# The u and v projections of a transformer mixer as one product in seven parts, with another order of the projections, the Fourier stage and attention

## The chip, the cores and the metric

The kernel runs on one core of a Trainium2 chip. The metric is the device time of one execution in microseconds (us). The engines are TensorE (PE, matmuls), VectorE (DVE), ScalarE (ACT), GpSimd (POOL, here an issuer of DMAs) and SyncE (SP, an issuer of DMAs). Each runs its own queue of instructions in order and waits on semaphores of the others. Matmuls write to eight banks of PSUM, 128 x 512 float32 each.

## The reference, cut to what matters

x is 512 x 1024 (512 tokens on an 8 x 64 grid). Two layers, each of them a half SwiGLU step, a mixer, and another half SwiGLU step; at the end a norm.

```python
def mixer(h, w_in, gate_bias, rpb, w_na_out, w_f_out, w_o):
    z = h @ w_in                     # h = rms_norm(x, g), 512 x 1024
    q, k, v, uf = z[..., :512], z[..., 512:1024], z[..., 1024:1536], z[..., 1536:2048]
    ga, gf = z[..., 2048:3072], z[..., 3072:]
    y_na = neighbourhood_attention(q, k, v, rpb) @ w_na_out   # 8 heads of 64, softmax over a window
    y_f = fourier_mix(uf) @ w_f_out  # per group of 128 channels: real part of the 2-D DFT
    g_na, g_f = sigmoid(ga + gate_bias[0]), sigmoid(gf + gate_bias[1])
    return (g_na * y_na + g_f * y_f) @ w_o
```

## The kernel before, in words

**Precision.** Every operand of a large matmul is split in a high part (in a rounded type, made by ACT, `hi`) and a low part (the rest, made by DVE, `lo`). A product is three matmuls: high by high, high by low, low by high. `mm3` (L285 to L288) is this for one tile; `late_low` (L439 to L450) puts the matmuls with the weights' low parts behind the others of a granule. `split` (L290 to L296) makes the two parts.

**Weights.** `Stream` and `Item` (from L151) bring the weights as granules of 128 x 1024 in a fixed order. SP loads a granule (`raw`), up to eight granules ahead (`FETCH`); some have a second granule added to them by an accumulating DMA of POOL or by a sum on DVE (L160). ACT makes `whi` (L175), DVE makes `wlo` (L178); three buffers each. `prep` stays two granules ahead of PE.

**Products in seven parts.** The feed-forward steps, the gates and the output projection split a 2 x 2 block product in Strassen's way: seven products of block sums in place of eight. A `product` (L447 to L450) takes two granules and writes a pair of PSUM banks: 24 matmuls of 512 columns. `snap` (L517) copies a pair of banks to SBUF on ACT, `less` (L522) subtracts such a copy on DVE. `ORDER` is the order 1, 5, 2, 6, 7, 3, 4.

**Norm.** The class `Norm` turns x by transposes (bank `tr`) and multiplies by the gain in four quads (`quad`: half of the channels by half of the tokens). The factor 1/rms of a token is `r` (`rstd`, L422 and L423, `rsqrt`, L304 to L309); it is applied after the products. `spread` writes r to DRAM and reads it back as a row on all partitions (`R`), which q and k need, since their tokens lie along the columns.

**The mixer** (`stage_mixer`), all in one order on PE:

- `proj_U`: u for the first 256 tokens, and for the last 256 tokens mirrored. For the mirror ACT and DVE copy the activations in reverse (`flip`, L986 and L987). 48 + 48 matmuls of 512 columns. Then sums and differences of the two halves, each split.
- `proj_V`: 96 matmuls of 512 columns in four banks, out by a split with r (L295, L296).
- `four_pos` four times: the Fourier transform along the positions, 12 matmuls of 256 columns each. DVE multiplies the bank by two rows of factors (L1048, L1049), adds and subtracts halves (L1050, L1051), and the result is split (L292, L293).
- `proj_q(0)`, `proj_k(0)`: `proj_T`, 24 matmuls of 512 columns each; DVE multiplies by R (L970), then a split (L292 and L293, or L295 and L296 for q).
- `four_ch` four times: the transform along the channels, two banks for each group, 6 matmuls. ACT copies the second bank (`fq`, L1063), DVE adds it to and takes it from the first (L1065, L1067), then a split (L1071, L1072).
- `proj_q(1)`, then for the head pairs `att_next`, `proj_k`, `att_outs`, `proj_q`: `att_next(hp)` transposes the probabilities of the pair before (L1140), makes the scores of this one (L1104), and calls `att_probs`: minimum of negated scores with the bias added on DVE (L1118), exponentials with sums on ACT (L1124), reciprocals on DVE (L1127), scaled copies on ACT (L1131).
- `f_some(n)`: n of the eight rows of the Fourier branch's output product, 12 matmuls each, which are put between the attention's parts.
- The gates and the output projection in seven parts each.

**What sets the order.** Within one engine the order is fixed when the program is built: a scheduler takes what is ready by its own estimate, except where `manual_schedule` keeps the order of the code for the named engines and `high_priority` draws a step ahead. [...] A pool gives out the banks of PSUM, and a matmul that starts a new content of a bank waits for the last reader of the old one. `constants` (L944) puts the loads of the Fourier matrices and factors on POOL's queue.

Of the kernel before, what the change touches and what calls it, by code (L numbers as in the profile page):

```python
# [40 lines left out]
def _granules():  # L41
# [7 lines left out]
    for l in range(L):  # L49
        for w in (1, 2):  # L50
# [36 lines left out]
def encoder_kernel(  # L87
# [95 lines left out]
    def stage_items():  # L183
# [5 lines left out]
        def strassen(s, name, idx, sizes, order, dma=False):  # L189
# [7 lines left out]
            for m in order:  # L197
                for g in range(len(sizes)):
# [7 lines left out]
                    elif m == 4:  # L206
                        add(d2[g])
                    elif m == 5:
                        add(d)
                    elif m == 6:  # L210
                        add(d, a, then=b.key if dma else None)
                    else:
                        add(c)

# [15 lines left out]
        for l in range(L):  # L230
# [4 lines left out]
            for name, n in (("u", 4), ("v", 4), ("qk", 8), ("f", 4)):  # L235
                for g in range(n):
                    add(Raw((s, name, g)))
# [11 lines left out]
    class Stream:  # L249
        def __init__(self):  # L250
            self.items = stage_items()
            self.pos = self.loaded = self.prepped = 0
            self.stage = 0

# [6 lines left out]
        def prep(self, to):  # L261
            n = len(self.items)
            while self.prepped < min(to, n) and self.items[self.prepped].stage <= self.stage:
                self.fetch(self.prepped + FETCH)
# [4 lines left out]
        def enter(self, stage):  # L269
            self.stage = stage  # L270
            self.fetch(self.prepped + FETCH)
# [40 lines left out]
    class Norm:  # L312
# [40 lines left out]
        def quad(self, i, j):  # L353
            self.tiles(i)
            js = slice(j * 256, (j + 1) * 256)
            hq, lq = self.h[i][:, :, js], self.l[i][:, :, js]
            if not self.mix:
                raw = self.raw[i, j] = slot(F32, "xr")
            for k2 in range(2):
# [11 lines left out]
            if not self.mix:  # L371
                split(hq, lq, raw)
# [45 lines left out]
        def rstd(self):  # L418
# [6 lines left out]
            if self.mix:  # L425
                pc = bank()
                PE.matmul(pc[:, 0:2], mirror, self.r[:, 3:1:-1], start=True, stop=True)
                self.rflip = small("rflip", 2)
                V.tensor_copy(self.rflip, pc[:, 0:2])
# [3 lines left out]
            V.tensor_tensor(self.r2, self.r, self.r, ALU.mult)  # L433

# [85 lines left out]
    def less(ps, t):  # L520
        for b in range(2):
            V.tensor_tensor(t[:, b, :], ps[b], t[:, b, :], ALU.subtract)  # L522

    def stage_ffn(norm, nxt, late):
# [27 lines left out]
        norm.tiles(1)  # L552
# [16 lines left out]
        acts = {1: (hx[0], lx[0], 0), 2: (hx[1], lx[1], 0), 3: (hx[1], lx[1], 256), 4: (*t4, 0)}  # L569

        def combine(m):

            if m == 5:
                V.tensor_tensor(raw[0, 0], raw[0, 0], raw[0, 1], ALU.subtract)
                acts[5] = parts(raw[0, 0], "t1")
            elif m == 7:
                V.tensor_tensor(raw[0, 1], raw[0, 1], raw[1, 1], ALU.subtract)
                acts[7] = parts(raw[0, 1], "t3")
            elif m == 6:
                V.tensor_tensor(raw[0, 0], raw[1, 1], raw[0, 0], ALU.add)  # L580
                acts[6] = parts(raw[0, 0], "t2")
            else:
                V.tensor_tensor(raw[1, 0], raw[1, 0], raw[0, 0], ALU.subtract)
                split(*t4, raw[1, 0])
# [230 lines left out]
        for i, (m, c, _) in enumerate(steps):  # L815
# [16 lines left out]
            if m == 4 and c == 0 and not late:  # L832
                with tc.manual_schedule(engines={mybir.EngineType.DVE, mybir.EngineType.Activation}):
                    make(i + 2)
                    nxt.quad(1, 1)
                    nxt.quad(0, 1)
# [94 lines left out]
    def stage_mixer(l, norm, nxt):  # L931
        mp = mix_pool[0]

# [22 lines left out]
        def wide():  # L956

            wh, wl = ws.next()
            for k in range(2):
                c = slice(k * T, (k + 1) * T)  # L960
                yield wh[:, c], wl[:, c]

        def proj_T(scale):
# [5 lines left out]
            t = tmp(s="q")  # L969
            V.tensor_tensor(t, ps, R, ALU.mult)  # L970
            hi, lo = hilo("q")
            split(hi, lo, t, scale)
            return hi, lo

        def proj_U():
            pss = [bank() for _ in range(4)]

            def straight(kt, wh, wl):
                for c in range(2):
                    lh, ll = [z[:, c * P : (c + 1) * P] for z in xs[kt]]  # L980
                    mm3(pss[c], lh, ll, wh, wl, kt == 0, kt == DT - 1)

            def mirrored(kt, wh, wl):
                flip = tmp(F32R, s="flip")
                xh, xl = [z.bitcast(F32) for z in xs[kt]]
                S.activation(flip[:, 0:256], xh[:, 511:255:-1], AF.Copy)  # L986
                V.tensor_copy(flip[:, 256:512], xl[:, 511:255:-1])  # L987
                for c in range(2):
                    lh, ll = [flip[:, z + c * P : z + c * P + P] for z in (0, 256)]
                    mm3(pss[2 + c], lh, ll, wh, wl, kt == 0, kt == DT - 1)  # L990

            for g in range(2):
                for k, w in enumerate(wide()):
                    straight(2 * g + k, *w)
                    mirrored(2 * g + k, *w)
                if g == 0:
                    norm.settle()
            w = [*wide(), *wide()]
            for kt in range(4):
                mirrored(4 + kt, *w[kt])  # L1000
            for kt in range(4):
                straight(4 + kt, *w[kt])
            norm.rstd()
            norm.spread(R)
# [645 lines left out]
```

## Time and profile before

| | |
|---|---|
| median of 3 runs | 1905.43 us (1904.45 to 1906.28) |
| profiled execution | 1906.04 us |
| its span in the trace | 1904.2 us |
| mean granted clock of PE | 0.999 |
| matmuls | 9189 |
| DMA | 364.36 MB, 191 GB/s over the span |
| mixer of layer 0: first matmul of u | 336.99 us |
| first position transform | 381.67 us |
| first scores | 406.76 us |
| first gate product | 492.51 us |

The span runs from the first to the last instruction in the trace; the profiled execution is the time of the same run from outside. In rows of the timeline the first number is the start in the span, the second the length of one instruction or group; matmuls overlap, so what a matmul costs is the distance to the next start. The end of a row says what ended the idle time ahead of it.

### The profile page before, as it was taken

The numbers are of one execution on the slowest core, as the hardware profiler recorded it, in microseconds if no ns is written. First come the engines' busy times: TensorE is split into PE (matmuls) and PEld (weight loads), VectorE is DVE, ScalarE is ACT, GpSimd is POOL, SyncE is SP. The second block draws the span as 40 slices with busy tenths as digits, with TensorE's granted clock in tenths as the row PEclk, the third lists the DMA queues.
The fourth block names the chain that finished last, engine by engine and source line by source line (L and its number), as shares of the span: only waits on it lengthen the run. The fifth ranks groups of instructions, "written<-read, shape, count | busy, mean of one in ns | idle before, by whom it ended". The sixth has DMA issues, their size and how long they took to land.

```text
span 1904.2 us, 25091 instructions
## 1 busy us (share of the span) xinstructions
PE 1891.7 (99%) x9189; PEld 1586.8 (83%) x9189; DVE 1602.4 (84%) x2000; ACT 1161.6 (61%) x1676; POOL 160.7 (8%) x198
## 2 busy tenths in 40 slices
PE   9999999999999999999999999999999999999998
PEld 7888888888888888888888888888888888888886
DVE  7877899586889987889997778995769899787899
ACT  6655665468566755566665556663675576555655
POOL 0101010000111010001010100100001101000010
PEclk9999999999999999999999999999999999999999
DMA  8776499323886776649877664992247867766594
GB/s 301 202 207 187 150 249 320 105 84 104 217 218 166 180 195 204 177 152 262 251 185 210 187 180 152 268 339 74 68 130 215 215 170 175 207 177 177 170 275 147
DMA packets 104636, 364.36 MB, mean 191 GB/s; under 512 B 12032, under 2 KB 12160, under 8 KB 104512
## 3 DMA queue, kind: packets, MB, share of 16 engines
q1 hardware_dynamic: 77568, 270.70, 40.1%
q0 software_dynamic: 26800, 92.04, 26.8%
q8 instruction: 72, 1.18, 0.2%
q14 instruction: 52, 0.43, 0.1%
q10 hardware_dynamic: 144, 0.02, 0.0%
HBM read 357.46 MB, written 2.11 MB: 189 GB/s over the span
## 4 chain that ended last, share of the span: by engine, by line
PE 95%; issue 2%; DMA 2%; DVE 1%; ACT 0%; POOL 0%; DVEq 0%; ACTq 0%; POOLq 0%; SPq 0%
PE A L447 9%; PE A L448 9%; PE A L450 9%; PE o L448 7%; PE o L447 7%; PE o L450 7%; PE ps L286 5%; PE ps L288 5%; PE ps L287 5%; PE B L448 4%; PE B L447 4%; PE B L450 4%; PE C L448 2%; PE C L447 2%; PE C L450 2%; PE tr L540 2%
## 5 line engine op out<-in xcount | busy, mean ns | idle before, releaser
L175 ACT ACTIVATE whi<-raw 128x1024 fp32r<-128x1024 f32 (+1 forms) x528 | 546.1, 1037 | 423.4 <-PE A L448 123.2
L178 DVE TENSOR_TENSOR wlo<-raw,whi 128x1024 fp32r<-128x1024 f32 (+1 forms) x528 | 627.3, 1193 | 191.2 <-ACT whi L175 186.5
L146 POOL DMA_DIRECT2D raw<-in_wst_dram x158 | 136.2, 873 | 1440.2 <-DMA raw<-in_wst_dram 674.7
L160 DVE TENSOR_TENSOR raw<-raw,raw 128x1024 f32<-128x1024 f32 (+1 forms) x146 | 172.6, 1191 | 1.2
L448 PE MATMUL A<-whi,xl 128*128 128x512 f32 x384 | 149.5, 389 | 0.0
L447 PE MATMUL A<-whi,xh 128*128 128x512 f32 x384 | 149.4, 389 | 0.0
L450 PE MATMUL A<-wlo,xh 128*128 128x512 f32 x384 | 110.5, 389 | 0.0
L170 ACT ACTIVATE whi<-raw 128x1024 fp32r<-128x1024 f32 (+1 forms) x79 | 81.6, 1036 | 40.2 <-PE A L448 12.4
L171 DVE SCALAR_TENSOR_TENSOR wlo<-raw,whi 128x1024 fp32r<-128x1024 f32 (+1 forms) x79 | 93.1, 1193 | 12.2 <-ACT whi L170 12.2
L633 ACT ACTIVATE th<-sn,rh 128x512 f32<-128x512 f32 x80 | 56.8, 714 | 69.4 <-DVE sn L522 69.4
L517 ACT ACTIVATE sn<-A 128x512 f32<-128x512 f32 x96 | 56.4, 589 | 51.3 <-PE A L450 51.2
L450 PEld LDWEIGHTS A<-wlo,xh 128*128 128x128 f32 x384 | 72.1, 188 | 15.0
L448 PEld LDWEIGHTS A<-whi,xl 128*128 128x128 f32 x384 | 72.1, 188 | 14.8
L447 PEld LDWEIGHTS A<-whi,xh 128*128 128x128 f32 x384 | 72.1, 188 | 14.8
L447 PE MATMUL B<-whi,t1h 128*128 128x512 f32 x192 | 76.2, 397 | 0.0
L447 PE MATMUL A<-whi,t3h 128*128 128x512 f32 x192 | 75.3, 392 | 0.4 <-ACT sn L517 0.4
L447 PE MATMUL C<-whi,xh 128*128 128x512 f32 x192 | 74.9, 390 | 0.0
L447 PE MATMUL A<-whi,t2h 128*128 128x512 f32 x192 | 74.9, 390 | 0.0
L448 PE MATMUL B<-whi,t1l 128*128 128x512 f32 x192 | 74.8, 390 | 0.0
L448 PE MATMUL A<-whi,t3l 128*128 128x512 f32 x192 | 74.8, 390 | 0.0
L448 PE MATMUL C<-whi,xl 128*128 128x512 f32 x192 | 74.7, 389 | 0.0
L448 PE MATMUL A<-whi,t2l 128*128 128x512 f32 x192 | 74.7, 389 | 0.0
(409 smaller groups left out, 4748.2 us busy)
## 6 DMA issues: line engine op xcount, KB each, us to landing
raw<-in_wst_dram SPq DMA_DIRECT2D x466, 512.0 KB, 5.4
raw<-in_wst_dram POOLq DMA_DIRECT2D x162, 512.0 KB, 7.9
raw<-in_wst_dram SPq DMA_DIRECT2D x30, 256.0 KB, 3.9
bm<-in_bias_dram SPq DMA_DIRECT2D x16, 384.0 KB, 6.0
vs<-v SPq DMA_DIRECT2D x12, 256.0 KB, 4.9
x<-in_xin_dram SPq DMA_DIRECT2D x4, 512.0 KB, 10.2
raw<-in_wst_dram POOLq DMA_DIRECT2D x8, 256.0 KB, 8.7
dft<-in_dft_dram POOLq DMA_DIRECT2D x8, 256.0 KB, 6.2
```

The costliest lines, as they stand in the source:

```text
L146: G.dma_start(out=self.t, in_=wst[GRAN_AT[self.plus]][:, 0 : self.n], accum_op=ALU.add)
L160: V.tensor_tensor(self.raw.t, self.raw.t, self.add.t, ALU.add)
L170: S.activation(hi, t, AF.Copy, scale=-1.0)
L171: self.last = V.scalar_tensor_tensor(lo, t, -1.0, hi.bitcast(F32), ALU.mult, ALU.subtract)
L175: S.activation(hi[:, cs], t[:, cs], AF.Copy)
L178: self.last = V.tensor_tensor(lo[:, cs], t[:, cs], hi[:, cs].bitcast(F32), ALU.subtract)
L286: PE.matmul(ps, lh, rh, start=start, stop=False, skip_group_check=again)
L287: PE.matmul(ps, lh, rl, start=False, stop=False, skip_group_check=again)
L288: PE.matmul(ps, ll, rh, start=False, stop=stop, skip_group_check=again)
L447: PE.matmul(ps, lh, rh, start=start, stop=False, skip_group_check=again)
L448: PE.matmul(ps, ll, rh, start=False, stop=False, skip_group_check=again)
L450: PE.matmul(ps, lh, rl, start=False, stop=stop, skip_group_check=again)
```

## The change

1. u and v are one block product in seven parts. The 2 x 2 blocks are halves of the channels by halves of the tokens on one side, and halves of the channels by (u, v) on the other. The granules `ua` to `ud` take the place of the eight granules of u and v. Order of the products: 1, 5, 6, 2, 7, 3, 4.
2. The granules of q0, k0 and q1 stand behind those of products 5, 6 and 2; PE computes these projections there. A projection now gives back a function for its second step (the product by R and the high part) and one for its third (the low part).
3. Inside `proj_UV`, DVE and ACT keep the order of the code. The low part of quad (0,1) is put off to after product 1.
4. The mirror is taken after the product: for each of two blocks, two matmuls of the split u (`uh`, `ul`) with a rounded mirror matrix.
5. k1 and q2 follow, then the position transforms, scores of pair 0, k2, the channel transforms, q3, and the rest of attention. Of the f rows, one stands ahead of `att_next(2)`, two and one around `att_outs(1)`, and one less on each side of `att_outs(3)`.
6. A quad now goes through float32 (`raw`) for the mixer too: four scaled copies on ACT, one conversion for the high part, one subtraction on DVE for the low.
7. `combos` holds the combinations of the feed-forward steps and of the mixer in common.

```diff
@@ stage_items @@
-            for name, n in (("u", 4), ("v", 4), ("qk", 8), ("f", 4)):
-                for g in range(n):
-                    add(Raw((s, name, g)))
+            qk = [(s, "qk", g) for g in range(8)]
+            strassen(s, lambda q: "u" + q, 0, two, (1, 5, 6, 2, 7, 3, 4), True, behind={5: qk[0:1], 6: qk[1:2], 2: qk[2:3]})
+            for key in qk[3:] + [(s, "f", g) for g in range(4)]:
+                add(Raw(key))
...
@@ Norm.quad_high @@
-                    if self.mix:
-                        split(hq[:, kt, :], lq[:, kt, :], tr[:, k, :], self.gain(4 * i + kt))
-                    else:
-                        S.activation(raw[:, kt, :], tr[:, k, :], AF.Copy, scale=self.gain(4 * i + kt))
-            if not self.mix:
-                split(hq, lq, raw)
+                    S.activation(raw[:, kt, :], tr[:, k, :], AF.Copy, scale=self.gain(4 * i + kt))
+            S.activation(hq, raw, AF.Copy)
+            return lambda: V.tensor_tensor(lq, raw, hq.bitcast(F32), ALU.subtract)
...
@@ combos @@
+        def combine(m):
+            p, a, b, op = {
+                5: ((0, 0), (0, 0), (0, 1), ALU.subtract),
+                7: ((0, 1), (0, 1), (1, 1), ALU.subtract),
+                6: ((0, 0), (1, 1), (0, 0), ALU.add),
+                4: ((1, 0), (1, 0), (0, 0), ALU.subtract),
+            }[m]
+            V.tensor_tensor(raw[p], raw[a], raw[b], op)
+            yield
+            if m != 4 or not t4:
+                acts[m] = (slot(F32R, f"t{m}h"), slot(F32R, f"t{m}l"), 0)
+            h, l, _ = acts[m]
+            S.activation(h, raw[p], AF.Copy)
+            yield
+            V.tensor_tensor(l, raw[p], h.bitcast(F32), ALU.subtract)
+            yield
...
@@ stage_mixer @@
-        def proj_U():
...
-        def proj_V():
...
+        def proj_UV():
+            acts, combine = combos(norm, None)
+            ws.depth = 8
+            with tc.manual_schedule(engines={mybir.EngineType.DVE, mybir.EngineType.Activation}):
+                steps = {m: combine(m) for m in (5, 6, 7, 4)}
...
+                step(5)
+                pa = pair("A")
+                product(pa, acts[1], K4, True, hook=lambda: step(5, 2))
+                norm.rstd()
+                norm.spread(R)
+                ws.prep(ws.pos + 3)
+                low10 = norm.quad_high(*norm.due.pop(0))
+                s1 = snap(pa)
+                norm.low01()
+
+                def second():
+                    low10()
+                    step(6, 2)
+
+                pb = pair("B")
+                product(pb, acts[5], K4, True, hook=second)
+                sb = snap(pb)
+                step(6)
+                q0 = proj_T(DH**-0.5)
+                step(7, 2)
+                product(pa, acts[6], K4, False, again=True, hook=lambda: step(7))
+                s2 = snap(pa)
+                k0 = proj_T(None)
+                step(4, 2)
+                q0 = q0()
+                step(4)
+                pc = pair("C")
+                product(pc, acts[2], K4, True)
+                q[0] = q0()
+                q1 = proj_T(DH**-0.5)
+                k0 = k0()
+                less(pc, s1)
+                k[0] = k0()
+                norm.flip()
+                product(pa, acts[7], K4, False, again=True)
+                q1 = q1()
+                constants()
+                less(pa, sb)
+                q[1] = q1()
+                product(pb, acts[3], K4, False, again=True)
+            ws.depth = FETCH
+            less(pb, s2)
+            uh, ul = slot(F32R, "uh", (2, T)), slot(F32R, "ul", (2, T))
+            split(uh, ul, s2)
...
+            product(pa, acts[4], K4, False, again=True)
...
+            for c in range(2):
+                pm = bank()
+                PE.matmul(pm, mir, uh[:, 1 - c, :], start=True, stop=False)
+                PE.matmul(pm, mir, ul[:, 1 - c, :], start=False, stop=True)
...
-        u = proj_U()
-        vt = proj_V()
+        u, vt = proj_UV()
...
-        for g in range(4):
-            four_pos(g)
-        proj_q(0)
-        proj_k(0)
-        for g in range(4):
-            four_ch(g)
-        proj_q(1)
...
-        for hp in range(3):
-            att_next(hp)
-            bias_for(hp + 1)
-            proj_k(hp + 1)
-            if hp:
-                att_outs(hp - 1)
-            if hp < 2:
-                proj_q(hp + 2)
+        proj_k(1)
+        proj_q(2)
+        for g in range(4):
+            four_pos(g)
+        att_next(0)
+        bias_for(1)
+        proj_k(2)
+        for g in range(4):
+            four_ch(g)
+        proj_q(3)
+        att_next(1)
+        bias_for(2)
+        att_outs(0)
+        proj_k(3)
+        f_some(1)
+        att_next(2)
+        bias_for(3)
         f_some(2)
+        att_outs(1)
+        f_some(1)
...
         swap_pools(0)
-        f_some(2)
+        f_some(1)
         next(first)
         att_outs(3)
         t12, _ = next(first)
         ws.prep(ws.pos + 2)
-        f_some(1)
```

More of the change, by code (lines that the diff above doesn't have):

```diff
@@ L187, in add, with strassen @@
             items.append(Item(*a, stage=st, **k))
-        def strassen(s, name, idx, sizes, order, dma=False):
+        def strassen(s, name, idx, sizes, order, dma=False, behind=None):
             def key(q, g):
@@ L213, in strassen @@
                         add(c)
+                for key in (behind or {}).get(m, ()):
+                    add(Raw(key))
         def out_sizes(c):
@@ L425, in rstd @@
             if self.mix:
[L426 to L429, printed above, removed]
                 return
@@ L433, in rstd, with flip @@
             V.tensor_tensor(self.r2, self.r, self.r, ALU.mult)
+        def flip(self):
+            pc = bank()
+            PE.matmul(pc[:, 0:2], mirror, self.r[:, 3:1:-1], start=True, stop=True)
+            self.rflip = small("rflip", 2)
+            V.tensor_copy(self.rflip, pc[:, 0:2])
         def spread(self, R):
@@ L968, in proj_T @@
                 mm3(ps, wh[:, c], wl[:, c], *xs[kt], kt == 0, kt == DT - 1)
[L969 to L973, printed above, removed]
-        def proj_U():
[L976 to L1004, printed above, removed]
-            constants()
-            outs = []
@@ new lines, in proj_T, with step, v_out @@
+            return out
+        def proj_UV():
[3 more added lines that the diff above has]
+                steps = {m: combine(m) for m in (5, 6, 7, 4)}
+                def step(m, n=1):
+                    for _ in range(n):
+                        next(steps[m])
+                step(5)
[40 more added lines that the diff above has]
+            split(uh, ul, s2)
+            vt = [None] * 4
+            def v_out(c, src):
+                t = vt[c] = slot(F32R, "v", (2, T))
+                split(t[:, 0, :], t[:, 1, :], src, norm.r[:, c : c + 1])
+            for b in range(2):
+                v_out(2 + b, sb[:, b, :])
+            product(pa, acts[4], K4, False, again=True)
+            us = []
+            S.activation(mir, mirror, AF.Copy)
@@ L1568, in _weights @@
         wo = g["mix_w_o"][l]
+        four("u", 0, u, 0, v, 0)
         four("w", 0, wo, 0, wo, T)
```

102 lines of the change are left out of this document (53 added, 49 removed).

## The prediction

> **What bounds the kernel now.** I read the busy shares and the chain first, from the page of the kernel before.
>
> ```profile
> span 1904.2 us, 25091 instructions
> ...
> PE 1891.7 (99%) x9189; PEld 1586.8 (83%) x9189; DVE 1602.4 (84%) x2000; ACT 1161.6 (61%) x1676; POOL 160.7 (8%) x198
> ...
> PE 95%; issue 2%; DMA 2%; DVE 1%; ACT 0%; POOL 0%; DVEq 0%; ACTq 0%; POOLq 0%; SPq 0%
> ```
>
> TensorE (PE) is busy for 1891.7 of 1904.2 us and makes up 95% of the chain. The view of waits for PE says how much it stands:
>
> ```profile
> PE ps L132 <- ACT warm L129: 2.7, 1, 2.7
> PE A L447 <- ACT sn L517: 0.4, 2, 0.2
> ```
>
> That is all: 2.7 us ahead of the first matmul and 0.4 us later. So a matmul that goes is time saved, and a wait of PE that comes is time lost at full price, as nothing on PE's path takes up slack. The other engines are read from windows around the mixer of layer 0: the products of u and v; the Fourier stage and attention; the gates.
>
> ```profile
> 336.99:381.20 44.21, 44.21 (x201) 36.71 (x200) 21.73 (x46) 18.01 (x31) 4.55 (x8) 1.00 0.24 79
> 381.20:492.50 111.30, 111.30 (x667) 96.35 (x666) 83.22 (x194) 74.51 (x175) 3.45 (x4) 1.00 0.40 118
> 492.50:625.00 132.50, 132.30 (x605) 108.86 (x604) 119.89 (x125) 84.65 (x108) 14.63 (x17) 1.00 0.76 197
> ```
>
> Columns after the length are PE, PEld, DVE, ACT, POOL, clock, DMA share and GB/s. In the first window DVE works 21.73 of 44.21 us and DMA 0.24: there is room for more work at the head. In the second they seem half idle too, but there single chains decide, not sums.
>
> **Matmuls removed.** Each projection of a layer takes 8 x 4 x 3 = 96 matmuls of 512 columns for v and 48 + 48 for u, straight and mirrored: 192. After it stand seven products of 24, so 168, and 4 matmuls against the mirror matrix: 172. The projections of q and k only move.
>
> ```profile
> 337.22 0.39 PE L287 MATMUL ps<-wlo,xh 128*128 128x512 f32 x1
> 337.44 0.39 PE L288 MATMUL ps<-whi,xl 128*128 128x512 f32 x1
> ...
> 381.67 0.28 PE L286 MATMUL ps<-dft,u 128*128 128x256 f32 x1
> 381.78 0.28 PE L287 MATMUL ps<-dft,u 128*128 128x256 f32 x1
> ...
> 398.10 0.39 PE L288 MATMUL ps<-xh,wlo 128*128 128x512 f32 x1
> 398.33 0.28 PE L286 MATMUL ps<-b,ch 128*128 128x258 f32 x1
> ...
> 406.76 1.69 PE L1104 MATMUL ps<-q,q 64*128 64x256 f32 x24
> 408.38 0.50 PE L286 MATMUL ps<-xh,whi 128*128 128x512 f32 x1
> ```
>
> Starts, not durations, count, because matmuls overlap. 512 columns go by in 0.227 us (0.22 to 0.23 between these starts), 256 in 0.12. So 20 fewer are 4.54 us a layer, **-9.08 us** in the two layers. That is the most the change can give, 0.48%.
>
> **The head: new work on DVE and ACT.** DVE gains per layer six weight lows, two weight sums, four combinations and their lows, six subtractions of 512 (3.9 us) and the low of u, and loses the mirrored copies and some smaller quad lows. That is net about 19 us: 6.8 + 2.3 + 9.1 + 3.9 + 1.1 - 2.4 - 1.9, the large ones at the 1.13 us between these starts.
>
> ```profile
> 342.31 0.16 DVE L307 TENSOR_TENSOR rt<-r 128x4 f32<-128x4 f32 x1
> 342.51 0.16 DVE L308 SCALAR_TENSOR_TENSOR rt<-rt,ms 128x4 f32<-128x4 f32 x1
> ...
> 384.51 1.22 DVE L178 TENSOR_TENSOR wlo<-raw,whi 128x1024 fp32r<-128x1024 f32 x1
> 385.64 0.42 DVE L1050 TENSOR_TENSOR bt<-m,m 128x256 f32<-128x256 f32 x1
> 385.98 0.42 DVE L1051 TENSOR_TENSOR bt<-m,m 128x256 f32<-128x256 f32 x1
> ```
>
> 21.7 + 19 would fit in the stretch, which grows by the 16 us of q0, k0 and q1. The order that the change writes down is what makes two waits. (1) The low of quad (0,1) is postponed; ahead of it in DVE's queue stand the low of product B's second granule (free at about 343.8), the 13 small operations of rstd (0.20 apart: 2.6), a weight sum and the low of q0's weights: 343.8 + 2.6 + 3 x 1.14 = 349.8. q0's second matmul would be due at 337.0 + 5.44 (A) + 0.87 (transposes) + 5.44 (B) + 0.23 = 349.0: 0.85 us late. (2) The low of combination 6 comes behind the low of quad (1,0), the combination, a sum, and a weight low that itself awaits two ACT conversions of about 1: ready at 356.4, wanted at 355.4 after the first delay: 1.0 late. Later products had margins of 0.1 us and more. I take **1.85 us a layer, +3.7**; bounds 0 and 3 a layer, since each margin stems from a ledger of a dozen steps.
>
> Transfers: u and v came as 8 loads of SP; now as 10, and 6 accumulating ones of POOL.
>
> ```profile
> raw<-in_wst_dram SPq DMA_DIRECT2D x466, 512.0 KB, 5.4
> raw<-in_wst_dram POOLq DMA_DIRECT2D x162, 512.0 KB, 7.9
> ```
>
> By the places of their issues and these times I estimate that the accumulations for product 6 land about 330, the broadcast of r about 361; they are wanted at 337 and later, and at 366. The Fourier constants, now queued on POOL behind product 7, have over 20 us. I price transfers at nothing; the DMA share of 0.24 covers them.
>
> **The main point: q3 behind the Fourier stage.** Let E be the end of q2 on PE. There PE has the position transforms (48 x 0.12 = 5.75), scores of pair 0 (1.62), k2 (5.45) and the channel transforms (24 x 0.12 = 2.87): q3 would start at E + 15.7. But its PSUM bank is that of the first group's channel product, which is read by ACT's copy `fq`. In ACT's queue, that `fq` comes behind the entire softmax of pair 0. Before, the channel transforms preceded these scores, and `fq` preceded the softmax. The rows of this chain, all from before:
>
> ```profile
> 383.30 0.69 DVE L1048 TENSOR_TENSOR m<-ps,rot 128x512 f32<-128x512 f32 x1
> 383.91 0.68 DVE L1049 TENSOR_TENSOR m<-ps,rot 128x512 f32<-128x512 f32 x1
> ...
> 393.64 0.42 DVE L1051 TENSOR_TENSOR bt<-m,m 128x256 f32<-128x256 f32 x1
> ...
> 398.53 0.69 DVE L970 TENSOR_TENSOR q<-ps,R 128x512 f32<-128x512 f32 x1 [1.53 <-PE ps L288]
> ...
> 399.39 1.23 DVE L178 TENSOR_TENSOR wlo<-raw,whi 128x1024 fp32r<-128x1024 f32 x1 [0.17 <-ACT whi L175]
> 400.54 0.69 DVE L293 TENSOR_TENSOR q<-q,q 128x512 fp32r<-128x512 f32 x1
> ...
> 409.81 0.42 DVE L1118 CUSTOM_DVE_ANT_0 s<-ps,bm 128x256 f32<-128x256 f32 x1
> ```
>
> A projection that ends like k0 (next start 398.33) has DVE's product by R at +0.2, the next weight low at +1.06 and DVE free at +2.2. Then come, in the written queue, 8 products by the rotation (0.60 between starts), 8 sums of 256 (0.34), 3 lows (0.6) and the lows of k1 and q2 (0.6): 4.8 + 2.7 + 1.8 + 1.2 = 10.5, so the first minimum of the scores starts at E + 12.7. Before, the same stretch from 383.30 to the last sum at 393.64 took 10.3 with one weight low in place of these two.
>
> ```profile
> 399.27 0.36 ACT L1063 ACTIVATE fq<-ps 128x255 f32<-128x255 f32 x1
> ...
> 410.33 0.51 ACT L1124 ACTIVATE s<-s,nmx 128x256 f32<-128x256 f32 x1 [2.04 <-DVE nmx L1118]
> ...
> 417.49 0.62 ACT L292 ACTIVATE q<-q 128x512 fp32r<-128x512 f32 x1
> 418.01 1.04 ACT L175 ACTIVATE whi<-raw 128x1024 fp32r<-128x1024 f32 x1
> ```
>
> ACT's first exponential follows a minimum by 0.52, and from it to the end of the q high took 418.01 - 410.33 = 7.68. After: first exponential at E + 13.35 (the last Fourier high is just ahead), a weight high in the midst (0.95), 7.68, then `fq` (0.36): E + 22.35. q3 waits 22.35 - 15.7 = 6.65 us a layer, **+13.3** for two. In it lie the waits of the channel products themselves: their banks come free behind the minima and the product by R, the last at about E + 17.1, so they end at E + 17.45. Bounds: 5.6 and 7.7 a layer. Nothing repays this wait: the transposes of pair 0 come after q3 and would find their softmax done either way.
>
> At the gates, the f rows that lay between the last attention outputs and the n rows are used up earlier.
>
> ```profile
> 478.88 0.40 PE L286 MATMUL ps<-whi,y 128*128 128x512 f32 x1
> ...
> 492.70 1.22 DVE L171 SCALAR_TENSOR_TENSOR wlo<-raw,whi 128x1024 fp32r<-128x1024 f32 x1
> ```
>
> Those rows began at 478.88, with the outputs done; the low of the second gate granule ended at 493.92, 15.0 later. With a row of 2.7 us less in between, A's second granule wants it at about 14.5: **0.5 us a layer, +1.0**, bounds 0 and 2.
>
> **The clock after such a wait.** One place in the trace shows a PE that has stood:
>
> ```profile
> 2.73 4.02 PE L132 MATMUL ps<-warm 128*128 128x512 bf16 x9 [2.73 <-ACT warm L129]
> ...
> 7.40 0.63 PE L447 MATMUL cl<-whi,xh 128*128 128x512 f32 x1
> 7.83 0.63 PE L448 MATMUL cl<-whi,xl 128*128 128x512 f32 x1
> ...
> 8.63 0.40 PE L448 MATMUL cl<-whi,xl 128*128 128x512 f32 x1
> ```
>
> Starts are 0.43 apart until 8.6, against 0.227 later: for 5.9 us, 47% of the time was lost, 2.8 us. Behind q3's wait, with 4.9 us of it unbroken, this could recur: 0 at one end, 2.8 at the other. The start's idle has the chip's own start in it; on the other hand the new idle is longer than its 2.73 us. I take half, **+2.8** for both layers.
>
> [...]
>
> **Sum.** 1906.04 (the profiled execution; 1904.2 of span and 1.84 around it) - 9.08 + 3.7 + 13.3 + 1.0 + 2.8 = 1917.8. The median of the runs, 1905.43, is 0.6 lower: **1917.2 us**, 0.6% slower.
>
> **Rivals.** (a) q3 does not wait, and the kernel is faster. Place: the `fq` of group 0 on ACT. It decides at E + 15.7: the first exponential would have to start by E + 6.7. The scores exist at E + 7.4 at the earliest, which speaks against it; only a queue order other than the written one would do, or a bank free sooner. Price -13.3 and -2.8: 1901.1, and 1896.4 without the head's and the gates' waits. Chance 0.06. (b) Part of the wait, 3 us a layer, and a smooth head, no cold clock: 1906.04 - 9.08 + 6 + 1 - 0.6 = 1903.4. Chance 0.05. (c) DVE falls behind at the head for good: each of the seven products 1.5 us late instead of two of them by 1. For: +19 us on DVE in one order; against: its idle 22 us of 44. 1917.2 + 2 x (10.5 - 1.85) = 1934.5. Chance 0.07. (d) The clock falls at both waits in full: 1920.0, chance 0.22. [...] (e) It never falls: 1914.4, chance 0.20. Between them lies the forecast, 0.40.
>
> **How the numbers follow.** Cases with q3's wait (d, e, forecast) hold 0.82. Low end: waits at 5.6, no other cost: 1906.0 - 9.1 + 11.2 - 0.6 = 1907.5; high end: 1906.0 - 9.1 + 15.4 + 6 + 4 + 5.6 - 0.6 = 1927.3. Range 1907 to 1927, leaving out (a), (b), (c). A measurement of this kernel can tell about 0.2%, 3.8 us, from no change. Slower than 1909.2: (c), (d), (e), the forecast, less 0.02 for the lowest corner, 0.87; within: (b) and that corner, 0.07; faster than 1901.6: (a), 0.06.
>
> **What would show it.** In the waits of PE, a projection's `ps` released by ACT `fq`, two times, some 5 us each; gaps at the channel products released by DVE; the first exponential of pair 0 13.3 us after q2; two waits of about 1 us at the first q projection and the third product; matmul starts 0.43 apart behind q3's wait if the clock falls. Without a wait on `fq` the forecast is wrong by 13 us or more, and if more than two products of the head wait, (c) holds.

## The result and the profile after

The changed kernel takes 1921.64 us (median of 4 runs, 1920.18 to 1922.47) against 1905.12 for the kernel before: a ratio of 1.0085, 95% interval 1.0068 to 1.0103. It is slower by 16.5 us. The profiled execution has a span of 1920.1 us, 15.9 more than before. The forecast was 1917.2, in a range of 1907 to 1927.

From the page of the changed kernel, the busy shares and the chain:

```profile
span 1920.1 us, 25083 instructions
...
PE 1891.3 (98%) x9149; PEld 1582.3 (82%) x9149; DVE 1642.9 (86%) x2006; ACT 1188.7 (62%) x1704; POOL 171.6 (9%) x210
...
PE 87%; ACT 4%; DVE 4%; issue 2%; DMA 2%; POOL 0%; DVEq 0%; ACTq 0%; POOLq 0%
```

The 40 matmuls are gone (9189 to 9149), but PE is busy about as long as before, 1891.3 us, in good part because some matmuls ran at half the clock, as shown below; and ACT and DVE now have 4% each of the chain. DVE works 40 us more in the kernel, 20 a layer. The view of waits for PE names the places (us in total, times, longest):

```profile
PE ps L293 <- ACT fq L1129: 9.1, 2, 4.5
PE ps L135 <- ACT warm L132: 2.7, 1, 2.7
PE A L457 <- ACT sn L527: 2.0, 2, 1.6
PE A L458 <- DVE t6l L559: 1.4, 2, 0.7
PE ps L294 <- DVE wlo L181: 1.3, 2, 0.7
PE ps L293 <- DVE rs L1192: 1.0, 2, 0.5
PE ps L294 <- DVE xl L379: 0.9, 2, 0.5
```

But for the warm-up, every wait shown here comes twice, once a layer. The largest is that of q3 on `fq`. Its chain stands in the timelines of the three engines, which I put side by side. PE first: the first position transform (E, the end of q2), the first and the last of the channel products, q3, and q3's next matmuls:

```profile
406.40 0.28 PE L293 MATMUL ps<-dft,u 128*128 128x256 f32 x1
...
419.43 0.28 PE L293 MATMUL ps<-b,ch 128*128 128x258 f32 x1
...
424.06 0.28 PE L295 MATMUL ps<-b,ch 128*128 128x256 f32 x1
428.88 0.80 PE L293 MATMUL ps<-xh,whi 128*128 128x512 f32 x1 [4.54 <-ACT fq L1129]
429.48 0.63 PE L294 MATMUL ps<-xl,whi 128*128 128x512 f32 x1
429.91 0.63 PE L295 MATMUL ps<-xh,wlo 128*128 128x512 f32 x1
```

DVE frees itself for the Fourier stage, then starts the scores' first minimum; ACT's first exponential, the end of its softmax, and `fq`:

```profile
408.61 0.68 DVE L1114 TENSOR_TENSOR m<-ps,rot 128x512 f32<-128x512 f32 x1
...
419.21 0.42 DVE L1183 CUSTOM_DVE_ANT_0 s<-ps,bm 128x256 f32<-128x256 f32 x1
```

```profile
419.87 0.50 ACT L1189 ACTIVATE s<-s,nmx 128x256 f32<-128x256 f32 x1
...
427.94 0.62 ACT L1001 ACTIVATE q<-q 128x512 fp32r<-128x512 f32 x1
428.46 0.64 ACT L1129 ACTIVATE fq<-ps 128x255 f32<-128x255 f32 x2
```

With E at 406.40: DVE free at E + 2.2, the first minimum at E + 12.8, the first exponential at E + 13.5, q3 at E + 22.5. Behind 419.43 the channel products need 2.87 us, so q3 was due at 422.30 and came 6.58 late. Then its matmuls start 0.43 apart, not 0.227. The view of windows shows the clock in three stretches of 3.41 us (busy time of PE first after the length; the last three columns are clock, DMA share and GB/s):

```profile
423.67:427.08 3.41, 0.62 (x3) 0.41 (x3) 1.48 (x4) 3.41 (x13) 0.00 (x0) 1.00 0.55 201
427.08:430.49 3.41, 1.60 (x4) 1.32 (x5) 1.77 (x6) 2.45 (x7) 0.00 (x0) 0.50 0.00 0
430.49:433.91 3.42, 3.42 (x10) 2.65 (x9) 3.21 (x13) 2.11 (x5) 0.00 (x0) 0.50 0.00 0
```

The clock is 1.00, 0.50, 0.50. After a stretch in which PE worked 0.62 of 3.41 us, the clock was half for 6.83 us. The first 1.8 us of that fell into the wait; q3 lost 2.5 us in layer 0 and 2.15 in layer 1.

### The profile page after: what moved, and what is told of

It is laid out like the page before. It is cut to its first block, busy times and chain, and to the rows that moved or that the text cites. A ratio compares the mean times of both kernels' runs of the same rounds, so it can differ in the third digit from the quotient of the medians.

```text
span 1920.1 us, 25083 instructions
## 1 busy us (share of the span) xinstructions
PE 1891.3 (98%) x9149; PEld 1582.3 (82%) x9149; DVE 1642.9 (86%) x2006; ACT 1188.7 (62%) x1704; POOL 171.6 (9%) x210
## 4 chain that ended last, share of the span: by engine, by line
PE 87%; ACT 4%; DVE 4%; issue 2%; DMA 2%; POOL 0%; DVEq 0%; ACTq 0%; POOLq 0%
PE A L458 9%; PE A L460 9%; PE A L457 9%; PE o L460 7%; PE o L458 7%; PE o L457 7%; PE B L457 5%; PE B L458 5%; PE B L460 5%; DMA raw<-in_wst_dram 2%; PE C L458 2%; PE C L457 2%; PE C L460 2%; PE ps L293 2%; PE ps L294 2%
## 5 line engine op out<-in xcount | busy, mean ns | idle before, releaser
L178 ACT ACTIVATE whi<-raw 128x1024 fp32r<-128x1024 f32 (+1 forms) x536 | 554.0, 1038 | 407.3 <-PE A L458 126.1
L181 DVE TENSOR_TENSOR wlo<-raw,whi 128x1024 fp32r<-128x1024 f32 (+1 forms) x536 | 636.4, 1194 | 163.1 <-ACT whi L178 161.9
L149 POOL DMA_DIRECT2D raw<-in_wst_dram x166 | 143.8, 878 | 1428.8 <-DMA raw<-in_wst_dram 769.4
L173 ACT ACTIVATE whi<-raw 128x1024 fp32r<-128x1024 f32 (+1 forms) x83 | 85.9, 1037 | 44.9 <-PE A L458 12.6
L458 PEld LDWEIGHTS A<-whi,xl 128*128 128x128 f32 x400 | 75.1, 188 | 15.5
L458 PE MATMUL C<-whi,xl 128*128 128x512 f32 x208 | 81.0, 389 | 0.0
L458 PE MATMUL B<-whi,xl 128*128 128x512 f32 x208 | 81.0, 389 | 0.0
L457 PE MATMUL B<-whi,xh 128*128 128x512 f32 x208 | 80.9, 389 | 0.0
L293 PE MATMUL ps<-xh,whi 128*128 128x512 f32 x128 | 52.3, 408 | 9.1 <-ACT fq L1129 9.1
L460 PE MATMUL C<-wlo,xh 128*128 128x512 f32 x208 | 59.8, 389 | 0.0
L460 PE MATMUL B<-wlo,xh 128*128 128x512 f32 x208 | 59.8, 389 | 0.0
L458 PE MATMUL A<-whi,t6l 128*128 128x512 f32 x136 | 52.9, 391 | 1.4 <-DVE t6l L559 1.4
## 6 DMA issues: line engine op xcount, KB each, us to landing
x<-in_xin_dram SPq DMA_DIRECT2D x4, 512.0 KB, 10.2
```

The costliest lines, as they stand in the source:

```text
L149: G.dma_start(out=self.t, in_=wst[GRAN_AT[self.plus]][:, 0 : self.n], accum_op=ALU.add)
L173: S.activation(hi, t, AF.Copy, scale=-1.0)
L178: S.activation(hi[:, cs], t[:, cs], AF.Copy)
L181: self.last = V.tensor_tensor(lo[:, cs], t[:, cs], hi[:, cs].bitcast(F32), ALU.subtract)
L293: PE.matmul(ps, lh, rh, start=start, stop=False, skip_group_check=again)
L457: PE.matmul(ps, lh, rh, start=start, stop=False, skip_group_check=again)
```

## The experiments

Each ran on a chip beside the kernel before. Medians, and ratio to the kernel before with its interval. The warm-up is left out of the last column:

| kernel | us | ratio (95%) | what PE waits for most, us in both layers |
|---|---|---|---|
| changed kernel | 1921.6 | 1.0085 (1.0068 to 1.0103) | `fq` 9.1 |
| order_only | 1926.0 | 1.0108 (1.0093 to 1.0123) | `fq` 9.1 |
| fq_dve | 1919.0 | 1.0075 (1.0059 to 1.0090) | `sn` at the gates 3.4, channel sums 3.0, lows of p 2.1 |
| ch_first | 1921.4 | 1.0083 (1.0068 to 1.0098) | softmax of pair 0 4.6 |
| ch_first_k3 | 1921.8 | 1.0087 (1.0071 to 1.0104) | weights at f and n rows 8.7 |
| two_in_head | 1912.9 | 1.0043 (1.0028 to 1.0058) | fourth Fourier high 2.9 |
| one_in_head | 1929.6 | 1.0131 (1.0115 to 1.0147) | combination 6 14.8 |
| prod_only | 1927.9 | 1.0117 (1.0101 to 1.0133) | combination 6 14.4, u 4.8 |
| two_newton | 1923.5 | 1.0091 (1.0074 to 1.0108) | product by R 8.4 |
| two_newton_b | 1927.4 | 1.0112 (1.0093 to 1.0131) | product by R 7.8 |
| one_at_5 | 1914.0 | 1.0039 (1.0026 to 1.0052) | nothing over 1.5 |
| two_b | 1912.3 | 1.0034 (1.0022 to 1.0046) | `sn` at the gates 1.7 |
| one_b | 1912.3 | 1.0040 (1.0028 to 1.0052) | nothing over 1.5 |

**Is it the order or the products?** order_only is the kernel before, with only the new order behind its own u and v:

```diff
+        proj_q(0)
+        proj_k(0)
+        proj_q(1)
+        proj_k(1)
+        proj_q(2)
         for g in range(4):
             four_pos(g)
-        proj_q(0)
-        proj_k(0)
+        att_next(0)
+        bias_for(1)
+        proj_k(2)
         for g in range(4):
             four_ch(g)
-        proj_q(1)
+        proj_q(3)
+        att_next(1)
...
```

> The kernel before with the new order alone: u and v as before, then q0, k0, q1, k1, q2 together, and from the position transforms on the order of the changed kernel. Theory: the wait of q3 and the lower clock behind it come from this order and not from the products: 1905.1 + 2 x 9.1 and about 1 to 2 us a layer at the n rows and gates: 1924 to 1927. Rival (the new DVE work of the products makes DVE late for the Fourier stage): no wait at q3, 1905 to 1908.

Measured 1925.97, inside the theory's range and 18 us from the rival's. Two waits of PE's list:

```profile
PE ps L286 <- ACT fq L1063: 9.1, 2, 4.5
PE A L447 <- ACT sn L517: 1.9, 2, 1.7
```

The first is the same wait to the tenth, with the old matmuls of u and v. So the order makes it, and the products are not needed for it. The second, at the gates, is there without the products too. The difference between the two kernels, 1926.0 against 1921.6, is what the products then gave net of their own waits: 4.4 us of the 9.1.

**Is it the place of `fq` in ACT's queue?** Two ways to take it out of there. fq_dve:

```diff
-            S.activation(qs[:, 1:256], p2[:, 1:256], AF.Copy)
+            V.tensor_copy(qs[:, 1:256], p2[:, 1:256])
```

> The changed kernel with one line changed: the copy fq of a channel product is made by DVE in place of ACT. Theory (the wait of q3 comes from the place of fq in ACT's queue, behind the whole softmax of pair 0): the bank is free once DVE has done its minima and the product by R, 17.5 us after the end of q2 in place of 22.2. q3 waits about 2 us a layer, not 6.6, the clock does not fall (2.5 us a layer), and some 1.5 us come back at the scores of pair 1, which wait for the last channel sums: 1921.6 - 2 x (4.6 + 2.5 - 1.5) = 1910.4, 1908 to 1912. Rival (there is simply too little matmul work between the Fourier stage and pair 1, so the wait only changes its place): 1918 to 1922, with the waits at the transposes of pair 0.

Measured 1918.98: the rival's range. q3 now starts behind the channel products with no wait of its own (it is 1.9 us later than due, for the waits inside the channel products, as expected). But PE, 5.5 us later:

```profile
429.08 1.91 PE L1205 MATMUL ps<-ident,s 128*128 128x128 f32 x16
430.92 1.10 PE L1169 MATMUL ps<-q,q 64*128 64x256 f32 x12
433.51 1.77 PE L1169 MATMUL ps<-q,q 64*128 64x256 f32 x12 [1.49 <-DVE fy L1133]
436.25 0.58 PE L293 MATMUL ps<-p,v 128*128 128x256 f32 x1 [0.97 <-DVE p L300]
```

The second scores of pair 1 wait for the channel sums and the attention outputs for the lows of p, both now late on DVE; and the clock falls here as it fell at q3, for 6.83 us in layer 0 and 3.41 in layer 1. The wait has moved by one step. At the gates 1.4 us of waits came on top of those of the changed kernel, and in layer 1 the clock fell there for 3.41 us, so the gain of 2.7 us is not all of one place. ch_first puts the channel transforms ahead:

```diff
         for g in range(4):
             four_pos(g)
-        att_next(0)
-        bias_for(1)
         proj_k(2)
         for g in range(4):
             four_ch(g)
+        att_next(0)
+        bias_for(1)
         proj_q(3)
```

> The changed kernel with the channel transforms put ahead of the scores of pair 0, behind k2. Theory in its narrow form (only the place of fq behind the softmax costs): the wait on fq goes, 1921.6 - 18 = 1904. Rival (too little matmul work as cover): the channel products wait some 2 us for the last Fourier low, and behind q3 PE has no work until the softmax of pair 0 is done, 27.7 us after q2 against 22.9 for the end of q3: about 7 us of waits a layer once more, with a lower clock behind or not: 1916 to 1922.

Measured 1921.37; the rival again. PE's transposes of pair 0, with what they waited for:

```profile
429.72 1.64 PE L1205 MATMUL ps<-ident,s 128*128 128x128 f32 x8 [0.35 <-ACT s L1196]
433.29 1.11 PE L1205 MATMUL ps<-ident,s 128*128 128x128 f32 x4 [1.93 <-ACT s L1196]
434.84 0.69 PE L1205 MATMUL ps<-ident,s 128*128 128x128 f32 x2
```

So the narrow theory falls: `fq` behind the softmax says where PE waits, not why it must. Between the position transforms and pair 1, DVE and ACT have a chain that is longer than the matmuls beside it, 21 us; whichever instruction comes last ends the wait. In ch_first the first position transform starts at 405.17 and the transposes that waited longest at 433.29: 28.1 us, with the same 21 us of matmuls in between.

**Does more cover help?** ch_first_k3 also draws k3 to behind q3, and an f row from each end of attention to the middle.

```diff
         proj_q(3)
+        proj_k(3)
         att_next(1)
         bias_for(2)
         att_outs(0)
-        proj_k(3)
-        f_some(1)
+        f_some(3)
         att_next(2)
...
```

> As the one before, and k3 moved up to behind q3, with three f rows in its place between pairs 1 and 2 and none around the last outputs. Rival of cover: the wait for the softmax of pair 0 goes, as q3 and k3 are 10.9 us of matmuls; about 2 us at the channel products and 1 to 3 us at the transposes of pairs 2 and 3 stay: 1921.6 - 2 x 7 + 3 = 1910, 1907 to 1913. Narrow theory of fq alone: no better than the kernel without k3's move, 1904, as its gain was had there.

Measured 1921.81, neither. The place between q3 and pair 1 is mended, with no wait at the transposes of pair 0. But the f rows and k3 are now missing near the gates, at the first n rows:

```profile
484.75 1.20 PE L293 MATMUL ps<-whi,o 128*128 128x512 f32 x4 [1.41 <-ACT whi L178]
488.14 0.79 PE L294 MATMUL ps<-wlo,o 128*128 128x512 f32 x1 [2.20 <-DVE wlo L181]
```

The clock falls there too, for 6.83 us in each layer. I had priced the missing cover at 1 to 3 us, at the transposes of pairs 2 and 3 and not here, and not the fall behind it. two_in_head brings cover from outside, by taking q1 out of the products:

```diff
-                q1 = proj_T(DH**-0.5)
...
+        proj_q(1)
         proj_k(1)
-        proj_q(2)
         for g in range(4):
             four_pos(g)
-        att_next(0)
-        bias_for(1)
-        proj_k(2)
+        proj_q(2)
         for g in range(4):
             four_ch(g)
+        att_next(0)
+        bias_for(1)
+        proj_k(2)
         proj_q(3)
         att_next(1)
```

> The products with q0 and k0 alone between them; behind them q1, k1, position transforms, q2, channel transforms, scores of pair 0, k2, q3, pair 1, and on as in the changed kernel. The theory is now that the stretch from the position transforms to pair 1 needs some 28 us of matmuls as cover for its DVE and ACT chain and has 21 in the changed kernel. Here it has 5.75 + 5.45 + 2.87 + 1.62 + 10.9 = 26.6. Waits a layer: 1.45 at the head, 1.6 at the last channel product, 0.5 at the transposes of pair 0, 1.8 at the n rows and gates; no fall of the clock: 1905.1 - 9.1 + 2 x 5.35 = 1906.7, 1904 to 1909. Rival (the products' DVE work, with one projection less between them, falls behind): above 1912.

Measured 1912.89: of the 16.5 us, 8.7 are gone, against 15 expected. The number lies in the range of the rival, whose mechanism is there in part only: the two waits at the head are 3.1 us in both layers together, against 2.3 in the changed kernel. Its trace has a span of 1911.0. The wait at the transposes of pair 0 is gone. The wait at the last channel product is there as expected, 1.5 us a layer, and in layer 0 the clock fell behind it, which I had not expected:

```profile
412.70:416.10 3.40, 1.93 (x15) 1.46 (x13) 3.28 (x8) 1.50 (x3) 0.00 (x0) 0.99 0.00 0
416.10:419.50 3.40, 3.40 (x22) 3.14 (x21) 3.19 (x13) 1.80 (x4) 0.00 (x0) 0.51 0.00 0
```

**Are the products a plain gain without the order?** prod_only has the products back to back and the old order behind them:

> The seven products alone, no projection between them, and behind them exactly the order of the kernel before. Theory: DVE's 38.5 us of work beside 38.1 us of matmuls make several waits of 1 us (3 to 5 a layer), and the first position transform waits about 5 us a layer for the last low of u, since nothing covers its making, with or without a fall of the clock: 1905.1 - 9.1 + 2 x (8 to 12) = 1912 to 1920. Rival (only the new order costs, the products are a plain gain): 1896 to 1899.

Measured 1927.85, above both ranges. one_in_head has q0 between the products, but behind product 6:

> As the one before, with q0 alone between the products and one projection more behind pair 1 (q3 and k3 there, one f row moved to the end). The tail has the cover that the kernel before had, and the head less: DVE's some 41 us of work stand against 43.6 us of matmuls there. Theory: waits of 2 to 4 us a layer at the head, under 1.5 at the attention: 1904 to 1911. If the head were free of waits with so little cover: 1900 to 1903.

Measured 1929.56. Both have the same large wait, from the timeline of one_in_head:

```profile
353.40 1.22 PE L457 MATMUL A<-whi,t6h 128*128 128x512 f32 x2 [5.10 <-ACT t6h L557]
356.74 0.79 PE L458 MATMUL A<-whi,t6l 128*128 128x512 f32 x1 [2.12 <-DVE t6l L559]
```

Product 6 comes straight behind product 5, and combination 6 needs the two quads whose lows and steps DVE still has to do. For prod_only the sum over DVE's 38.5 us said 3 to 5 us of waits a layer at the head; this one chain made 7.2, and the clock was at half for 6.8 us in layer 0 and 10.2 in layer 1 from there on (10.2 in both layers of one_in_head). one_at_5 tests this by moving q0 alone:

```diff
                 step(6)
+                q0 = proj_T(DH**-0.5)
                 step(7, 2)
                 product(pa, acts[6], K4, False, again=True, hook=lambda: step(7))
                 s2 = snap(pa)
-                q0 = proj_T(DH**-0.5)
```

> one_in_head with its one projection, q0, moved from behind product 6 to behind product 5. In one_in_head product 6 came straight behind product 5 and waited 5.1 us a layer for combination 6, and the clock fell behind it. Theory (it is that one place at the head that needs cover, 5.4 us of it): this wait goes but for the 0.9 that the changed kernel has there, and no other product waits over 1 us; at the tail the waits stay as in one_in_head, near 2.5 us a layer: 1905.3 - 9.1 + 2 x 5 = 1906, 1904 to 1909. Rival (DVE has too much work for one projection at the head, wherever it stands): the wait comes back at products 2 or 7, 1912 to 1925.

Measured 1913.98: 15.6 us came back by one move, so the place was right, but it is 5 us above its range. That is the range of the rival, but not its wait: in the profiled execution (1911.7, a span of 1909.5) no wait but the warm-up is over 1 us, and the clock does not fall in the mixer. The other three executions took 1913.9 to 1914.4, at a mean granted clock of 0.995 to 0.997 against 0.999, so in them it fell somewhere; no trace shows where.

**Can the rest be had?** two_newton moves the small Newton steps of rstd from DVE to POOL in two_in_head:

```diff
         for _ in range(3):
+            if pool:
+                G.tensor_tensor(t, r, r, ALU.mult)
+                G.tensor_tensor(t, t, ms, ALU.mult)
+                G.tensor_scalar(t, t, -0.5, 1.5, ALU.mult, ALU.add)
+                G.tensor_tensor(r, t, r, ALU.mult)
+                continue
             V.tensor_tensor(t, r, r, ALU.mult)
...
-                self.r = rsqrt(ms, 4)
+                self.r = rsqrt(ms, 4, self.mix)
```

> two_in_head with the nine Newton steps of the mixer's rstd as twelve small operations on POOL in place of DVE: 1.8 us of DVE's queue at the head go. Theory (the two waits at the head, 0.54 at q0 and 0.89 at product 6 in layer 0, 1.43 and some at layer 1, come from DVE's order there): both go, 1912.9 - 3.3 = 1909.6, 1908 to 1911. Rival: r comes later by POOL's slower steps, the product by R waits for R, and the low parts behind it are late: 1912 to 1916.

Measured 1923.48: the rival's mechanism at more than its price. Both waits at the head did go, but the twelve steps took 12.3 us on POOL (345.13 to 357.48), r went out to DRAM at 357.78 in place of 345.5, and DVE stood 10.56 us for R:

```profile
345.13 1.09 POOL L315 TENSOR_TENSOR rt<-r 128x4 f32<-128x4 f32 x1 [19.75 <-DVE r L312]
346.30 1.06 POOL L316 TENSOR_TENSOR rt<-rt,ms 128x4 f32<-128x4 f32 x1
```

```profile
375.81 0.69 DVE L1004 TENSOR_TENSOR q<-ps,R 128x512 f32<-128x512 f32 x1 [10.56 <-DMA R<-row]
```

Eight of these twelve operations of 128 x 4 took 1.04 to 1.09 us in layer 0 and the other four 0.19 to 0.68, against 0.16 on DVE. two_newton_b adds a higher priority for the Fourier evacuation:

```diff
-            V.tensor_tensor(m1, ps, rots[0], ALU.mult)
...
+            with tc.high_priority():
+                V.tensor_tensor(m1, ps, rots[0], ALU.mult)
...
```

> two_newton with a higher priority in the scheduler for the position transforms' evacuation, so that the high part of the fourth group no longer stands behind ACT's copy fq of the first. In two_in_head that wait was 1.5 us a layer, and behind it the clock fell for some 3.3 us, 1.7 lost. Theory: both go, another 2 x 3.2: 1903.2, 1901 to 1906. Rival (the wait moves on to the lows of the same groups, and the clock falls all the same): 1908 to 1911.

Measured 1927.39, under the same delay of R; the wait on the fourth Fourier high fell from 2.9 to 0.4 us, and 1.1 came up at the scores. two_b and one_b have that priority without POOL, and the lows of the n rows' weights ahead of one sum; two_b from two_in_head, one_b from one_at_5:

```diff
+        ws.prep(ws.pos + 2)
         t12, _ = next(first)
-        ws.prep(ws.pos + 2)
```

> two_in_head with the higher priority for the position transforms' evacuation, and the lows of the n rows' weights ahead of one sum. Theory: the wait of 1.5 us a layer on the fourth group's high part goes, and with it the fall of the clock behind it, 1.7: 1912.9 - 6.4 - 1 = 1905.5, 1903 to 1908. Rival (as two_newton_b hints, with 0.4 and 1.1 us left there: the wait moves to the scores, and the clock falls all the same): 1909 to 1912.

> one_at_5 with the same two edits as two_b. The tail has as much cover as in the kernel before. If all waits that are left are the 1.4 us a layer at the head, 1 at the tail and 1 at the gates: 1905.3 - 9.1 + 6.8 = 1903, 1901 to 1906. If the head has too little cover: above 1910.

Measured 1912.25 and 1912.27, both above their ranges and near the numbers of their rivals. The profiled executions are better than the medians, with spans of 1907.9 and 1909.7. The clock stays full in the mixer of two_b; in one_b it falls for 3.41 us in layer 0. The medians can't tell these kernels from two_in_head and one_at_5 at their intervals. No version beats the kernel before: at two_b's PE the waits that are left are

```profile
PE A L457 <- ACT sn L527: 1.7, 1, 1.7
PE A L458 <- DVE t6l L559: 1.4, 2, 0.7
PE ps L294 <- DVE wlo L181: 1.3, 2, 0.6
PE ps L1167 <- DVE fq L1126: 1.1, 2, 0.6
PE ps L294 <- DVE xl L379: 0.8, 2, 0.4
```

and behind the channel products, which begin at 412.25, the scores of the pair's two heads start late and no longer side by side:

```profile
415.74 1.48 PE L1167 MATMUL ps<-q,q 64*128 64x256 f32 x12
417.79 1.91 PE L1167 MATMUL ps<-q,q 64*128 64x256 f32 x12 [0.57 <-DVE fq L1126]
419.62 0.50 PE L293 MATMUL ps<-xh,whi 128*128 128x512 f32 x1
```

From 412.25 to 419.62 are 7.4 us where 2.87 + 1.62 would do, so 2.9 are lost, and as much in layer 1. The waits of the list are only 0.6 of it. In the changed kernel the two heads' scores start in twos, 0.004 us apart, and a new two every 0.12 us. One head's six took 0.98 us there. In two_b the groups of twelve took 1.48 and 1.91, so by an estimate from these lengths one head's six start 0.5 us behind the other's in the first group and 0.93 in the second. The likely reason, not tested, is that each head's bank comes free at its own time. The same stretch lost 3.0 us a layer in one_at_5, 3.1 and 2.9 in one_b, 4.1 and 3.2 in two_in_head. For two_b 5.8 us here and 5.2 of the other four waits of the list are more than the 9.1 us that the products gave, and its span is 3.7 longer than before.

## Why the prediction was right, and where its sizes were off

**Matmuls removed: right.** 40 fewer in the trace, 9.08 us by the unchanged 0.227.

**The main point, q3 behind the Fourier stage: right** in place, chain and price. 6.65 us a layer were forecast; 6.58 were measured in each. The steps at E + 2.2, 12.7, 13.35 and 22.35 stand in the trace at 2.2, 12.8, 13.5 and 22.5. order_only shows that this wait belongs to the order. But the forecast's rival (a), with 13.3 us to be had by another place of `fq`, was wrong: fq_dve and ch_first gained 2.7 and 0.3 us, neither clear of the runs' spread. "Nothing repays this wait" was right about the transposes with the wait in place; without it, they and the scores would have waited. The wait is one of cover, and the step that names a single instruction as its cause is too narrow. One reading was off as well: I called DVE and ACT half idle in the second window of the kernel before, but by its row DVE works 83.22 and ACT 74.51 of 111.30 us, so there was less room than I took.

**The head: right**, a bit high. Two waits, at q0 and product 6, of 0.54 and 0.87 us in layer 0 and 0.67 and 0.87 in layer 1: 2.95 us against 3.7. The rest of the estimate, that other products are in time, held, and DVE's added work, priced at 19 us a layer, came to 20. Transfers cost nothing there, but the reason given was thin: from 337 to 384 us the DMA share is 0.78 and not 0.24, and four accumulating loads from there took 15.0 us to land (median), where I had used 7.9.

**The clock: right that it falls, the size too small.** I took half of the price of the start, the middle of two ends and no mechanism; it fell at both waits, to 0.50 for 6.83 us each time. q3 lost 2.5 and 2.15 us, 4.65 in all, against 2.8. Rival (d), at 5.6, was nearer. How much idle brings it down is not shown. In two_in_head PE worked 1.93 of the 3.40 us before the fall in layer 0, with one unbroken wait of 1.47; the same wait in layer 1 lowered nothing. In one_b (layer 0) it even fell at 413.85, after a stretch of 3.41 us in which PE worked 2.84, so PE's busy time alone does not say when.

**The gates: the wrong instruction and too little.** I expected the low of the second gate granule. The first low of the n rows was late instead, by 0.8 us a layer. And product 7 of the first gate, 1.78 us late in layer 0 and 0.52 in layer 1, waited for `sn`, which stood on ACT behind a conversion that waited 2.1 us for its granule's DMA:

```profile
525.11 0.50 PE L457 MATMUL A<-whi,t3h 128*128 128x512 f32 x1 [1.62 <-ACT sn L527]
523.51 1.06 ACT L178 ACTIVATE whi<-raw 128x1024 fp32r<-128x1024 f32 x1 [2.10 <-DMA raw<-in_wst_dram]
524.47 0.58 ACT L527 ACTIVATE sn<-A 128x512 f32<-128x512 f32 x1
```

Before, the like wait was 0.37 a layer. So the term is 1.6 + 1.6 = 3.2 us against 1.0. I had priced no transfer at the gates at all. order_only has both waits with the old products, 1.9 us for `sn` behind a conversion that waited for its DMA and 1.3 for the lows, so they come with the order. What makes the granule land late is open: ch_first, with the same f rows, waits only 0.5 us for `sn`. Another 0.6 us came up near the end of the feed-forward step ahead of the mixer of layer 0, at a low of weights; I had taken it as free, and its cause is not tested.

**The sum.** -9.1 + 2.95 + 13.2 + 4.65 + 3.2 + 0.6 = +15.5 of the span's 15.9; 0.4 stay without a place. The forecast had +11.7; it was short by 1.9 at the clock, 2.2 at the gates, 0.6 ahead of the mixer, and 0.75 too much at the head.

## What to carry to other kernels

When matmuls are moved into a place that is short of them, ask which chain of the other engines they covered where they were: here 16 us of projections had hidden the Fourier stage and the first softmax, and every order that put them elsewhere paid at some new place. A wait that ends at one instruction is a matter of cover if taking that instruction away ends it at the next: try two ways of removal before a cause is named. Price a wait on PE with the fall of the clock that can follow it: behind q3's wait of 4.54 us it cost another 2.5 us in layer 0, while behind the 1.6 us at the gates of the changed kernel the clock stayed at 1.00. And where two short groups of matmuls share a time, look at their starts: the stretch with the scores lost 2.9 us in two_b, of which the list of waits shows 0.6.

## What the runs showed of the hardware beyond what was expected

- In the mixer the clock of PE went down to 0.50 for 3.41, 6.83 or 10.24 us at a time (10.24 in one_in_head and prod_only) and came back in one step. It fell after stretches of 3.4 us in which PE worked 0.62 us (changed kernel), 1.93 us (two_in_head, layer 0) and 2.84 us (one_b, layer 0), and not after the wait of 1.6 us at the gates of the changed kernel (1.00 from 505 to 530 us).
- Eight of the twelve operations of 128 x 4 on POOL in layer 0 of two_newton took 1.04 to 1.09 us, against 0.16 on DVE.
- Matmuls of 64 rows of two heads ran side by side: 24 scores took 1.69 us in the changed kernel, starting in twos 0.004 us apart. In two_b 12 took 1.48 us and the next 12 took 1.91.
